# Ten of sixteen conditioning vectors are computed among the mixers' projections, each in two halves of 32 matmuls

## The chip, the cores and the metric

One core of a Trainium2 chip runs the program. The metric is the device time of one execution in microseconds (us); a table gives it for three executions, and one further execution was profiled. Engines are named as the profile names them: PE (TensorE matmuls) and PEld (its weight loads), DVE (VectorE), ACT (ScalarE), POOL (GpSimd), and SP, whose queue issues nearly all DMAs, in order.

## The reference

Two layers of a diffusion-transformer block over 512 latent and 256 context tokens of width 1024. Each layer has three sublayers: feed-forward, mixer (differential attention, a state-space scan and a retention scan side by side) and feed-forward. A conditioning vector `c` (and `c_ctx` for the context) yields nine vectors of width 1024 per layer: shift, scale and gate of each sublayer.

```python
sc, scc = silu(c), silu(c_ctx)
for l in range(2):
    m_l = (sc @ ada_w[l] + ada_b[l]).reshape(b, 1, 3, 3, D)      # 9 vectors for the latent tokens
    m_c = (scc @ ada_w[l] + ada_b[l]).reshape(3, 3, D)           # 9 for the context tokens
    x  = residual(x,  0.5 * swiglu(x * (1 + m_l[0, 1]) + m_l[0, 0], ...), gate m_l[0, 2])   # sublayer 0
    xc = ... the same with m_c
    y_l, y_c = hybrid_mixer(x * (1 + m_l[1, 1]) + m_l[1, 0], ...)                           # sublayer 1
    x = residual(x, y_l, gate m_l[1, 2])
    x = residual(x, 0.5 * swiglu(x * (1 + m_l[2, 1]) + m_l[2, 0], ...), gate m_l[2, 2])     # sublayer 2
    # the context stream has sublayers 1 and 2 in the first layer only
```

Here `residual` is a layer norm of `alpha * x + (1 + gate) * sublayer`. One vector is a product of a 1024 x 1024 block of `ada_w` with two columns (latent and context).

## The kernel before

Six sublayers follow each other: `ffn(0,0)`, `mixer(0)`, `ffn(0,2)`, `ffn(1,0)`, `mixer(1)`, `ffn(1,2)`. Tiles come from pools with a fixed number of buffers per tag; a scheduler orders each engine's instructions, and each engine then runs its own list in order and waits on semaphores.

**Feed-forward.** 22 column blocks are taken as 11 pairs in the groups (0,1), (2,3), (4,5), (6,7), (8,9,10). For a pair, the gate and up weights (1 MB each) are loaded into a buffer of the tag `raw` (two buffers of 1 MB), some sums of blocks are formed on POOL, and ACT and DVE split each block into two float16 pieces (lines L320 and L321). PE then runs the gate and up products (L511, or L571 where the pair is done plainly), and at a group's end the down products (L743; L816 for the last group). Feed-forward of layer 1's last sublayer is wholly plain (L571, L772, L816).

**Mixer.** Projections of the input, 256 columns at a time, are *fill*: generators in a queue of jobs (`Fill`), which a list of pipelined steps (`Skew`) runs in small portions between the steps of the scans and of attention. `share` is the portion per step, the jobs' summed cost over the number of steps. Weights of a projection come by `unit()`, two names ahead of their use, through the same two `raw` buffers, and are split into blocks of a ring of 16. Projections write PSUM tiles of the tag `pf` (two buffers). At the end `merge` multiplies with `w_out` (its four blocks are the units `wo0` to `wo3`, their matmuls L1566).

**Conditioning vectors.** `ada_vec(l, v)` computes one. The two columns sit in `scT`, padded to 32, as the stationary operand; 128 rows of `ada_w` by 1024 columns are loaded per `k` (512 KB, tag `ada`, two buffers), and four matmuls of 256 columns write the four 32-row strips of one PSUM tile (L162; each float32 matmul is two records in the trace). After eight `k`, gates (v of 2, 5, 8) go to DRAM as rows, and the others are transposed on PE and written to `mT` by DVE. Vectors 0 and 1 of layer 0 are done in `first_pair` (in blocks of 128 columns, L639). The other sixteen are in `plan`: seven in `ffn(0,0)` and nine in `ffn(0,2)`, one ahead of each pair's products. The scheduler puts their matmuls between others as their loads land.

Of the kernel before, what the change touches and what calls it, by code (L numbers as in the profile page):

```python
# [8 lines left out]
F32 = mybir.dt.float32  # L9
# [34 lines left out]
def kernel(  # L44
# [110 lines left out]
    def ada_vec(l, v, alloc):  # L155

        pa = sm([P, 256], f"ada{l}_{v}")
        for k in range(KC):
            raw = alloc([P, D], f"adaw{l}_{v}_{k}")
            nc.sync.dma_start(out=raw, in_=ada_w[l, k * P:(k + 1) * P, v * D:(v + 1) * D])  # L160
            for j in range(4):
                PE.matmul(pa[32 * j:32 * j + 32, :], lhsT=scT[:, k, :], rhs=raw[:, j * 256:(j + 1) * 256],  # L162
                          start=(k == 0), stop=(k == KC - 1), tile_position=(0, 32 * j))
        rows = small.tile([P, 256], F32, tag="adar", name=f"adar{l}_{v}", bufs=1)
        if v % 3 == 2:
            mul = ISC if v == 5 else 0.5 * ISC
            G.memset(rows, 0.0)
            for r in range(2):
                nc.sync.dma_start(out=rows[r::32, :],
                                    in_=ada_b[l, v * D:(v + 1) * D].rearrange("(j f) -> j f", j=4))  # L170
            V.tensor_tensor(out=rows, in0=pa, in1=rows, op=ALU.add)
            V.tensor_scalar(out=rows, in0=rows, scalar1=mul, scalar2=mul, op0=ALU.mult, op1=ALU.add)
            row = dram.tile([2, D], F32, name=f"grow{l}_{v}")
            for r in range(2):
                nc.sync.dma_start(out=row[r].rearrange("(j f) -> j f", j=4), in_=rows[r::32, :])
            gate_rows[l, v // 3] = row
            return
        V.tensor_copy(rows, pa)
        pt = sm([P, 2, P], f"adat{l}_{v}")
        for h in range(2):  # L180
            PE.transpose(pt[:, h, :], rows[:, h * P:(h + 1) * P], ident)
        src = pt.rearrange("p h (j m) -> p h j m", m=32)
        dst = mT[l][:, v, :, :].rearrange("p (j h) r -> p h j r", h=2)
        bias = ab_cols[:, l, v * 8:v * 8 + 8].rearrange("p (j h) -> p h j", h=2)
        for h in range(2):
            V.tensor_tensor(out=dst[:, h], in0=src[:, h, :, 0:2],
                            in1=bias[:, h].unsqueeze(2).to_broadcast([P, 4, 2]), op=ALU.add)
# [169 lines left out]
    def ffn(l, i, uT, stream, ntiles, nxt, last, todo):  # L357
# [5 lines left out]
        with tc.tile_pool(name=f"ffn{l}{i}", bufs=1) as fp:  # L363
# [487 lines left out]
            for gi, prs in enumerate(GROUPS):  # L851
                for q in prs:
                    if todo and (q > 1 or len(todo) >= NPAIR - 1 - q):
                        ada_vec(*todo.pop(0), al("ada"))
# [70 lines left out]
    def mixer(l, uT, stream, nxt, last):  # L925
# [5 lines left out]
        with tc.tile_pool(name=f"mix{l}", bufs=1) as mp:  # L931
# [57 lines left out]
            pipe = Skew(fill)  # L989

# [601 lines left out]
            fill.add(1.3, ret_kt(1))  # L1592
            share = fill.left / 13
# [6 lines left out]
            for pr_ in range(2):  # L1600
                for n, t in enumerate(order_f):
                    if (pr_, n) == (0, 3):
                        fill.add(nout * TOK, gate_job("z", gate_ssm))
                        fill.add(ROT, qk_job(0))
                    pipe.push(ret_state(pr_, t), share)
# [6 lines left out]
            for h in range(2, 4):  # L1612
                fill.add(ROT, qk_job(h))
            fill.add(nout * TOK, gate_job("rg", gate_ret))
            share = fill.left / (3 * nout + LEAD)
            for h in range(4):
                for t in range(nout):
                    pipe.push(attend(h, t), share)
                    if (h, t) == (3, LEAD - 1):
                        merge_setup()  # L1620
# [4 lines left out]
            pipe.drain()  # L1625
        return mg["norm"]
# [7 lines left out]
    plan = {(0, 0): [(0, v) for v in range(2, 9)], (0, 2): [(1, v) for v in range(9)]}  # L1634
# [73 lines left out]
```

## Time and profile before

| | |
|---|---|
| device time, three executions | 2879.3, 2877.5, 2873.37 us (median 2877.5) |
| the profiled execution | 2878.8 us, of which 2877.0 are the span from first to last instruction |
| PE busy | 2656.4 us, 92% of the span |
| DVE busy | 2118.9 us, 74% |
| ACT, POOL busy | 1210.6 and 1160.1 us, 42% and 40% |
| mean granted TensorE clock | 0.973 of full |

Busy time is the union of an engine's instructions over the span, and the sublayers differ in what limits them, so the shares are averages. A granted clock below 1 means that PE ran part of the time at the lower of its two levels, 1.2 instead of 2.4 GHz.

### The profile page before, as it was taken

The numbers are of one execution on the slowest core, as the hardware profiler recorded it, in microseconds if no ns is written. First come the engines' busy times: TensorE is split into PE (matmuls) and PEld (weight loads), VectorE is DVE, ScalarE is ACT, GpSimd is POOL, SyncE is SP. The second block draws the span as 40 slices with busy tenths as digits, with TensorE's granted clock in tenths as the row PEclk, the third lists the DMA queues.
The fourth block names the chain that finished last, engine by engine and source line by source line (L and its number), as shares of the span: only waits on it lengthen the run. The fifth ranks groups of instructions, "written<-read, shape, count | busy, mean of one in ns | idle before, by whom it ended". The sixth has DMA issues, their size and how long they took to land. (4 is left out here: it accounts for less than half of the span.)

```text
span 2877.0 us, 42905 instructions
## 1 busy us (share of the span) xinstructions
PE 2656.4 (92%) x16415; PEld 1554.0 (54%) x16415; DVE 2118.9 (74%) x3134; ACT 1210.6 (42%) x2619; POOL 1160.1 (40%) x1016
## 2 busy tenths in 40 slices
PE   6899999989899988999999889988999899899998
PEld 4454555557677863544555444544555667744443
DVE  4967788786867688768877988879787768634455
ACT  3443344434436444533443344433433537333321
POOL 1744465241525455534552655446242425400011
PEclk8999999999999999999999999999999999999999
DMA  7635432333234244444453422221422333152330
GB/s 242 196 127 176 133 132 98 107 121 90 78 88 105 74 176 163 160 161 147 147 169 121 165 65 82 74 66 61 156 83 87 103 107 100 67 176 88 120 122 30
DMA packets 220355, 342.63 MB, mean 119 GB/s; under 512 B 16008, under 2 KB 162166, under 8 KB 220150
## 3 DMA queue, kind: packets, MB, share of 16 engines
q1 hardware_dynamic: 220150, 339.90, 36.6%
q8 instruction: 129, 2.11, 0.3%
q14 instruction: 76, 0.62, 0.1%
HBM read 301.43 MB, written 23.22 MB: 113 GB/s over the span
## 5 line engine op out<-in xcount | busy, mean ns | idle before, releaser
L511 PEld LDWEIGHTS <-pcgu 128*128 128x128 f16 x3792 | 373.4, 99 | 329.1 <-issue 93.3
L511 PE MATMUL ch<-T,pcgu 128*128 128x384 f16 x1920 | 337.0, 329 | 5.2 <-ACT U L518 5.2
L743 PEld LDWEIGHTS <-act 128*128 128x128 f16 x1512 | 142.9, 98 | 216.4 <-issue 58.4
L321 DVE SCALAR_TENSOR_TENSOR pcgu<-rawgu,pcgu 128x512 f16<-128x512 f32 x218 | 216.3, 1008 | 49.2 <-ACT pcgu L320 48.2
L571 PE MATMUL pl<-uT,pcgu 128*128 128x512 f16 (+2 forms) x1068 | 228.0, 367 | 7.7 <-DVE uT L214 7.0
L320 ACT ACTIVATE pcgu<-rawgu 128x512 f16<-128x512 f32 x218 | 133.9, 626 | 211.5 <-PE ds L743 126.6
L429 POOL TENSOR_TENSOR S4gu<-rawgu,S2gu 128x512 f32<-128x512 f32 x60 | 90.1, 1502 | 273.7 <-DVE pcgu L321 137.3
L571 PEld LDWEIGHTS <-pcgu 128*128 128x128 f16 x1236 | 121.8, 101 | 138.5 <-issue 24.7
L511 PEld LDWEIGHTS <-pegu 128*128 128x128 f16 x1248 | 122.2, 98 | 108.2 <-issue 29.7
L800 POOL TENSOR_TENSOR acc<-acc,gate 128x512 f32<-128x512 f32 x44 | 62.2, 1421 | 282.9 <-DVE acc L780 253.7
L743 PE MATMUL ds<-pcd,act 128*128 128x512 f16 x612 | 152.3, 381 | 4.3 <-DVE acc L749 2.8
L743 PE MATMUL dc<-pcd,act 128*128 128x512 f16 x576 | 149.1, 384 | 7.2 <-DVE acc L749 7.1
L976 PEld LDWEIGHTS <-uT 128*128 128x128 f16 x1344 | 134.7, 101 | 29.9 <-issue 8.4
L228 ACT ACTIVATE u<-pt,abc 128x128 f32<-128x128 f32 x224 | 81.2, 467 | 161.2 <-PE pt L225 98.9
L816 PE MATMUL pd<-pcd,act 128*128 128x512 f16 x594 | 141.1, 379 | 4.2 <-DVE dt L822 4.2
L321 DVE SCALAR_TENSOR_TENSOR pcd<-rawd,pcd 128x512 f16<-128x512 f32 x124 | 109.0, 893 | 40.6 <-ACT pcd L320 40.5
L426 POOL TENSOR_TENSOR S1gu<-rawgu 128x512 f32<-128x512 f32 x60 | 88.8, 1480 | 116.2 <-DMA rawgu<-in_ffn_w_gate_dram 55.8
L816 PEld LDWEIGHTS <-act 128*128 128x128 f16 x792 | 77.4, 98 | 99.2 <-issue 10.7
L458 DVE TENSOR_TENSOR act<-sg,act 128x384 f16<-128x384 f32 (+1 forms) x149 | 123.6, 873 | 3.3 <-ACT act L457 3.3
L94 POOL TENSOR_SCALAR rs<-mv 128x1 f32<-128x1 f32 x32 | 17.9, 559 | 263.3 <-DVE mv L273 263.3
L518 ACT COPY U<-ch 128x384 f32<-128x384 f32 x180 | 83.6, 472 | 76.8 <-PE ch L511 76.1
L428 POOL TENSOR_TENSOR S3gu<-rawgu 128x512 f32<-128x512 f32 x60 | 96.4, 1607 | 32.4 <-DVE pegu L321 16.2
(391 smaller groups left out, 6209.5 us busy)
## 6 DMA issues: line engine op xcount, KB each, us to landing
adaw<-in_ada_w_dram SPq DMA_DIRECT2D x128, 512.0 KB
rawd<-in_ffn_w_down_dram SPq DMA_DIRECT2D x44, 1024.0 KB
rawgu<-in_ffn_w_gate_dram SPq DMA_DIRECT2D x43, 1024.0 KB
rawgu<-in_ffn_w_up_dram SPq DMA_DIRECT2D x43, 1024.0 KB
row<-yh SPq DMA_DIRECT2D x56, 256.0 KB
rawwo<-in_w_out_dram SPq DMA_DIRECT2D x8, 1024.0 KB
xt<-row SPq DMA_DIRECT2D x32, 256.0 KB
gate<-grow SPq DMA_DIRECT2D x28, 256.0 KB
```

The lines of the kernel that those rows point to most:

```text
L320: A.activation(pc[:, 0], src, AF.Copy, scale=SW)
L321: V.scalar_tensor_tensor(out=pc[:, 1], in0=src, scalar=SW, in1=pc[:, 0], op0=ALU.mult, op1=ALU.subtract)
L426: G.tensor_tensor(out=s1, in0=a21, in1=a22, op=ALU.add)
L428: G.tensor_tensor(out=s3, in0=a11, in1=a21, op=ALU.subtract)
L429: G.tensor_tensor(out=s4, in0=a12, in1=s2, op=ALU.subtract)
L458: V.tensor_tensor(out=pc[:, 1], in0=src, in1=pc[:, 0], op=ALU.subtract)
L511: PE.matmul(pp, lhsT=wt[pr_][q][m][:, a, k, :], rhs=rhs, start=(n == 0 and m in (1, 2, 5)), stop=(n == 11), skip_group_check=m in (1, 6, 7 ...
L518: A.copy(t_, chain[q])
L571: PE.matmul(pp[:, j, o:o + hi - lo], lhsT=wp.at(a, k, cc * P, (cc + 1) * P), rhs=uT[:, b, k, lo:hi], start=(n == 0), stop=(n == KC * 3 - 1))
L743: PE.matmul(pd, lhsT=acts[q][m][:, a, ts], rhs=wd[q][m][:, b], start=(n == 0 and m in (1, 2, 5)), stop=(n == len(prs) * 3 - 1), skip_group ...
L816: PE.matmul(pd, lhsT=acts[q][2 * cc + hf][:, a, o:o + P], rhs=wd[q][2 * cc + h][:, b], start=(n == 0), stop=(n == len(prs) * 6 - 1))
L976: PE.matmul(pp, lhsT=uT[:, a, k, t * P:(t + 1) * P], rhs=pc.at(b, k, 0, n_), start=(n == 0), stop=(n == KC * 3 - 1))
```

## The change

Three things change together. `ada_vec` becomes a generator that works on halves of 512 columns: per half all weights are loaded first (`nk` row blocks per DMA), then 32 matmuls of 128 columns follow each other, and then the half is finished. In the feed-forward sublayers it is run at once with `nk = 2` (DMAs of 512 KB in the two `ada` buffers). In the mixers it is a fill job with `nk = 4` (DMAs of 1 MB in the two `raw` buffers, PSUM in `pf`). And `plan` now gives three vectors to `ffn(0,0)`, six to `mixer(0)`, three to `ffn(0,2)` and four to `mixer(1)`.

```diff
-    def ada_vec(l, v, alloc):
-        pa = sm([P, 256], f"ada{l}_{v}")
-        for k in range(KC):
-            raw = alloc([P, D], f"adaw{l}_{v}_{k}")
-            nc.sync.dma_start(out=raw, in_=ada_w[l, k * P:(k + 1) * P, v * D:(v + 1) * D])
-            for j in range(4):
-                PE.matmul(pa[32 * j:32 * j + 32, :], lhsT=scT[:, k, :], rhs=raw[:, j * 256:(j + 1) * 256],
-                          start=(k == 0), stop=(k == KC - 1), tile_position=(0, 32 * j))
...
+    def ada_vec(l, v, alloc, space, nk):
         for h in range(2):
+            c0 = v * D + h * 512
+            raws = []
+            for k in range(0, KC, nk):
+                raws.append(alloc([P, nk, 512], f"adaw{l}_{v}_{h}{k}"))
+                nc.sync.dma_start(out=raws[-1], in_=ada_w[l, k * P:(k + nk) * P, c0:c0 + 512]
+                                  .rearrange("(k p) f -> p k f", p=P))
+            yield 0.5
+            pa = space([P, P], f"ada{l}_{v}{h}")
+            for k in range(KC):
+                for j in range(4):
+                    PE.matmul(pa[32 * j:32 * j + 32, :], lhsT=scT[:, k, :],
+                              rhs=raws[k // nk][:, k % nk, j * P:(j + 1) * P],
+                              start=(k == 0), stop=(k == KC - 1), tile_position=(0, 32 * j))
+            yield 1.7
...
# ffn
-                        ada_vec(*todo.pop(0), al("ada"))
+                        for _ in ada_vec(*todo.pop(0), al("ada"), sm, 2):
+                            pass
...
# mixer
+            raw_of = lambda shape, nm: main.tile(shape, F32, tag="raw", name=f"raw{nm}", bufs=2)
+            told = set()
+            def ada_job(v):
+                yield from ada_vec(*v, raw_of, pf, 4)
+                told.add(v)
+            def add_ada(n):
+                for _ in range(min(n, len(todo))):
+                    fill.add(4.4, ada_job(todo.pop(0)))
...
             fill.add(1.3, ret_kt(1))
+            add_ada(1)
...
                         fill.add(ROT, qk_job(0))
+                        add_ada(1)
...
             for h in range(2, 4):
+                add_ada(1)
                 fill.add(ROT, qk_job(h))
             fill.add(nout * TOK, gate_job("rg", gate_ret))
+            add_ada(len(todo))
...
                     if (h, t) == (3, LEAD - 1):
+                        fill.until(lambda: needed <= told)
                         merge_setup()
...
             pipe.drain()
+            fill.until(lambda: not fill.jobs)
...
-    plan = {(0, 0): [(0, v) for v in range(2, 9)], (0, 2): [(1, v) for v in range(9)]}
+    plan = {(0, 0): [(0, v) for v in range(2, 5)], (0, 1): [(0, v) for v in range(5, 9)] + [(1, 0), (1, 1)],
+            (0, 2): [(1, v) for v in range(2, 5)], (1, 1): [(1, v) for v in range(5, 9)]}
```

**In the feed-forward sublayers** the scheduler still breaks the runs up. On PE, in the down products of pairs 2 and 3 of `ffn(0,0)`, before (`ada_5` is vector 5, `adaw_5_1` its second load):

```order
L743 MATMUL dc_11_2121<-pcd_2_1_1755,act_2_1_1693 128x512
L162 MATMUL ada_5_2677<-adaw_5_1_2684,scT 32x256
L162 MATMUL ada_5_2677<-adaw_5_2_2690,scT 32x256 x3
L743 LDWEIGHTS act_2_2_1696
L743 MATMUL ds_10_2120<-pcd_2_2_1758,act_2_2_1696 128x512
```

and in the same place of the change (`ada_41` is the second half of vector 4, `adaw_4_14` its load from row block 4 on):

```order
L748 MATMUL ds_10_2197<-pcd_2_2_1799,act_2_2_1737 128x512
L169 MATMUL ada_41_2465<-adaw_4_14_2461,scT 32x128 x2
L169 MATMUL ada_41_2465<-adaw_4_16_2463,scT 32x128 x5
L748 LDWEIGHTS act_2_2_1737
L748 MATMUL ds_11_2199<-pcd_2_2_1799,act_2_2_1737 128x512
```

Vector 5 and those after it have left this place. Over the whole program the vectors' matmuls stood in 121 runs before (52 in `ffn(0,0)`, 69 in `ffn(0,2)`) and stand in 110 now (31, 28 in `mixer(0)`, 32 in `ffn(0,2)`, 19 in `mixer(1)`).

**In the first mixer** PE had, between the transposes of the retention keys (`rkp`) and the gate projection (`pkz`):

```order
L1310 MATMUL rkp_0_7119<-mats,rrrk_0_6566 128x128 x3
L1188 MATMUL pst_0_6596<-xw_0_6594,bt_6331 128x256 x2
L976 LDWEIGHTS uT_5049
L976 MATMUL pkz_0_7147<-pcz_6365,uT_5049 128x256
L976 LDWEIGHTS uT_5049
```

and has now, with the first vector that moved here (vector 5 of layer 0):

```order
L1329 MATMUL rkp_0_6937<-mats,rrrk_0_6449 128x128 x3
L169 MATMUL ada_50_6951<-rawadaw_5_00_6942,scT 32x128 x16
L169 MATMUL ada_50_6951<-rawadaw_5_04_6944,scT 32x128 x16
L169 MATMUL ada_51_7052<-rawadaw_5_10_7044,scT 32x128 x16
L982 LDWEIGHTS uT_4934
```

48 matmuls stand ahead of the projection that followed at once before; the vector's last 16 come among the scan's next steps.

**On SP, at the end of the first mixer,** the loads of the last `w_out` blocks (`rawwo`) and of the next sublayer's first weights (`rawgu`) stood like this before:

```order
L337 DMA rawwo_9508<-in_w_out_dram 128x8x256
L1410 DMA qs_0_9008<-rpaq_0_9005 64x768 x2
L337 DMA rawgu_00_10694<-in_ffn_w_gate_dram 128x8x256
L1417 DMA ks_0_9077<-rpak_0_9074 64x2x768 x4
L243 DMA gbc_0_9526<-agb 128x1024
L337 DMA rawgu_01_10708<-in_ffn_w_up_dram 128x8x256
L243 DMA bbc_0_9528<-agb 128x1024
```

and now, with the loads of layer 1's vectors 0 and 1 (`rawadaw_0_10` is the second half of vector 0):

```order
L243 DMA bbc_0_9926<-agb 128x1024
L163 DMA rawadaw_0_10_9699<-in_ada_w_dram 128x4x512
L163 DMA rawadaw_0_14_9701<-in_ada_w_dram 128x4x512
L163 DMA rawadaw_1_00_9768<-in_ada_w_dram 128x4x512
L163 DMA rawadaw_1_04_9770<-in_ada_w_dram 128x4x512
L163 DMA rawadaw_1_10_9831<-in_ada_w_dram 128x4x512
L1572 DMA xr_0_10030<-row_0_5062 128x1024
L163 DMA rawadaw_1_14_9833<-in_ada_w_dram 128x4x512
L342 DMA rawwo_9892<-in_w_out_dram 128x8x256
L1572 DMA xr_0_10212<-row_1_5146 128x1024
L342 DMA rawwo_9906<-in_w_out_dram 128x8x256
```

Six loads of vectors now stand between the norm's rows and the last two `w_out` blocks, all in the two `raw` buffers.

## Rows read from the trace of the kernel before

**Rows 1.** The page's first part: busy us, share of the span, instructions.

```profile
PE 2656.4 (92%) x16415; PEld 1554.0 (54%) x16415; DVE 2118.9 (74%) x3134; ACT 1210.6 (42%) x2619; POOL 1160.1 (40%) x1016
```

**Rows 2.** First and last starts of L743 and L816 in `ffn(1,0)`: ns min/median/max, starts.

```profile
L743 PE MATMUL dc<-pcd,act x180: 377/379/632, 1688.8 to 2008.7; 128*128 128x512 f16 x180
...
L816 PE MATMUL pd<-pcd,act x162: 377/379/380, 2058.0 to 2144.9; 128*128 128x512 f16 x162
```

**Rows 3.** Busy time by windows: `ffn(0,0)`, `ffn(0,2)`, `ffn(1,0)`, first down product to last.

```profile
core 0: us, PE busy (x) PEld busy (x) DVE busy (x) ACT busy (x) POOL busy (x), PEclk, DMA share, GB/s
130.10:593.70 463.60, 443.56 (x2635) 228.94 (x2633) 364.86 (x495) 199.53 (x386) 219.49 (x158) 1.00 0.40 130
1126.80:1600.40 473.60, 456.52 (x2789) 232.01 (x2787) 363.12 (x498) 191.81 (x371) 219.23 (x159) 0.99 0.46 151
1688.80:2145.30 456.50, 418.80 (x2267) 223.62 (x2265) 367.58 (x471) 190.65 (x374) 215.00 (x155) 0.98 0.25 81
```

**Rows 4.** The same three windows, matmuls of the tile `ada` alone.

```profile
130.10:593.70 463.60, 31.39 (x360) 1.00 0.40 130
1126.80:1600.40 473.60, 44.13 (x512) 0.99 0.46 151
1688.80:2145.30 456.50, 0.00 (x0) 0.98 0.25 81
```

**Rows 5.** PE's waits in `ffn(1,0)`, 1645 to 2009: us, times, longest.

```profile
PE dc L743 <- DVE acc L749: 10.5, 7, 2.8
```

**Rows 6.** PE's timeline around runs of vector matmuls: start us, us, count of records.

```profile
37.03 0.93 PE L685 MATMUL pc_first<-uT_in,pcfirst 128*128 128x256 f16 x7
37.89 0.30 PE L639 MATMUL ada_first<-pcadaw_first,sc 128*32 128x128 f32 x2
...
39.56 0.28 PE L639 MATMUL ada_first<-adaw_first,sc 128*32 128x128 f32 x2
39.77 0.39 PE L685 MATMUL pc_first<-uT_in,pcfirst 128*128 128x256 f16 x2
...
96.38 0.64 PE L162 MATMUL ada<-adaw,scT 128*32 128x256 f32 x8
96.95 4.08 PE L511 MATMUL ch<-uT_in,pcgu 128*128 128x384 f16 x24
...
172.40 1.07 PE L162 MATMUL ada<-adaw,scT 128*32 128x256 f32 x16
173.40 0.82 PE L743 MATMUL dc<-ped,act 128*128 128x512 f16 x3
```

**Rows 7.** Groups of instructions by shape: the vectors' matmuls and their transposes.

```profile
L162 PE MATMUL ada<-adaw,scT 128*32 128x256 f32 x1024 | 88.5, 394 | 1.9 <-DMA adaw<-in_ada_w_dram 1.6
...
L181 PE MATMUL adat<-mats,adar 128*128 128x128 f32 x20 | 3.8, 273 | 0.0
```

**Rows 8.** Windows: `mixer(0)`, `mixer(1)`, and two stretches of `mixer(0)` (columns as rows 3).

```profile
594.00:1031.60 437.60, 412.17 (x3061) 318.82 (x3059) 325.98 (x589) 209.50 (x563) 169.52 (x225) 0.98 0.32 93
2145.30:2512.00 366.70, 338.05 (x2406) 251.33 (x2405) 273.16 (x487) 176.59 (x453) 137.25 (x175) 0.97 0.33 97
...
918.00:958.30 40.30, 35.06 (x256) 27.61 (x256) 30.93 (x61) 34.40 (x107) 22.48 (x40) 1.00 0.26 79
...
736.00:760.00 24.00, 15.96 (x105) 13.42 (x104) 23.07 (x43) 11.98 (x36) 13.21 (x16) 0.85 0.35 111
```

**Rows 9.** PE's waits in the mixers (594 to 1031, then 2145 to 2512).

```profile
PE sc L1434 <- ACT pe L1439: 5.4, 6, 3.0
PE pch L1242 <- DVE yo L1232: 5.2, 2, 4.5
...
PE pl L571 <- DVE uT L214: 7.0, 1, 7.0
```

**Rows 10.** From the chain that ended last: landings of 1 MB weight loads.

```profile
2500.55 5.28 DMA rawgu<-in_ffn_w_gate_dram
...
2530.69 11.13 DMA rawd<-in_ffn_w_down_dram
```

More of the change, by code (lines that the diff above doesn't have):

```diff
@@ L152, in condition @@
         nc.sync.dma_start(out=agb.rearrange("r (k p) -> (r k) p", p=P), in_=agb_sb)
-    def ada_vec(l, v, alloc):
-        pa = sm([P, 256], f"ada{l}_{v}")
-        for k in range(KC):
-            raw = alloc([P, D], f"adaw{l}_{v}_{k}")
-            nc.sync.dma_start(out=raw, in_=ada_w[l, k * P:(k + 1) * P, v * D:(v + 1) * D])
-            for j in range(4):
-                PE.matmul(pa[32 * j:32 * j + 32, :], lhsT=scT[:, k, :], rhs=raw[:, j * 256:(j + 1) * 256],
-                          start=(k == 0), stop=(k == KC - 1), tile_position=(0, 32 * j))
[L164 to L179, printed above, removed]
-        for h in range(2):
[L181 to L187, printed above, removed]
@@ new lines, in ada_vec @@
+    def ada_vec(l, v, alloc, space, nk):
+        for h in range(2):
+            c0 = v * D + h * 512
[12 more added lines that the diff above has]
+            yield 1.7
+            rows = small.tile([P, P], F32, tag="adar", name=f"adar{l}_{v}{h}", bufs=2)
+            if v % 3 == 2:
+                mul = ISC if v == 5 else 0.5 * ISC
+                G.memset(rows, 0.0)
+                for r in range(2):
+                    nc.sync.dma_start(out=rows[r::32, :], in_=ada_b[l, c0:c0 + 512].rearrange("(j f) -> j f", j=4))
+                V.tensor_tensor(out=rows, in0=pa, in1=rows, op=ALU.add)
+                V.tensor_scalar(out=rows, in0=rows, scalar1=mul, scalar2=mul, op0=ALU.mult, op1=ALU.add)
+                if h == 0:
+                    gate_rows[l, v // 3] = dram.tile([2, D], F32, name=f"grow{l}_{v}")
+                for r in range(2):
+                    nc.sync.dma_start(out=gate_rows[l, v // 3][r, h * 512:(h + 1) * 512]
+                                      .rearrange("(j f) -> j f", j=4), in_=rows[r::32, :])
+                continue
+            V.tensor_copy(rows, pa)
+            pt = space([P, P], f"adat{l}_{v}{h}")
+            PE.transpose(pt, rows, ident)
+            V.tensor_tensor(out=mT[l][:, v, 4 * h:4 * h + 4, :], in0=pt.rearrange("p (j m) -> p j m", m=32)[:, :, 0:2],
+                            in1=ab_cols[:, l, v * 8 + 4 * h:v * 8 + 4 * h + 4].unsqueeze(2).to_broadcast([P, 4, 2]),
+                            op=ALU.add)
@@ L922, in drain, with mixer @@
                 self.push()
-    def mixer(l, uT, stream, nxt, last):
+    def mixer(l, uT, stream, nxt, last, todo):
         need_ctx = l < DEPTH - 1
@@ L989, in mixer @@
             pipe = Skew(fill)
+            raw_of = lambda shape, nm: main.tile(shape, F32, tag="raw", name=f"raw{nm}", bufs=2)
[6 more added lines that the diff above has]
+                    fill.add(4.4, ada_job(todo.pop(0)))
+            needed = set(q for q in todo if q[0] == l and q[1] < 8)
             sv = sml([P, 4, 2, 4], "sv")
@@ L1639 @@
         if i == 1:
-            norm = mixer(l, uT, stream, nxt, last)
+            norm = mixer(l, uT, stream, nxt, last, todo)
         else:
```

## Prediction

> **What bounds the kernel now.** The page's first part comes first: PE is busy for 92% of the span and DVE for 74% [rows 1]. That makes PE the suspect everywhere, but the vectors move from one kind of sublayer to another, so the question is what a microsecond of PE work costs in each kind. The trace holds a comparison made for this. `ffn(0,0)`, `ffn(0,2)` and `ffn(1,0)` have the same six token tiles and the same products, and carry seven, nine and no vectors. I marked the same stretch in each, from the first down product to the last (for `ffn(1,0)` the starts 1688.8 and 2144.9 of [rows 2], the others alike), and read it by windows. Without vectors the stretch takes 456.5 us, and PE is busy for only 418.8 of them [rows 3]: there PE waits again and again for DVE, most of all for sums into the accumulator [rows 5]. With 31.4 us of vector matmuls it takes 463.6 us, with 44.1 us of them 473.6 [rows 3, 4]. So the first 31.4 us cost 7.1 us, 0.23 for one, and the next 12.7 cost 10.0, 0.79 for one. A feed-forward sublayer has room for some of this work, and not for all that it has now.
>
> The mixers are the other side. PE is busy for 412.2 of 437.6 us in the first and 338.1 of 366.7 in the second [rows 8]: 25.4 and 28.6 us are not used, of which 7.0 are one wait at the very end of the second, for the next sublayer's input [rows 9].
>
> **What one vector costs on PE.** In the timeline a run of 8 records (four float32 matmuls of 256 columns, one for each strip) holds PE from 96.38 to 96.95, 0.57 us; a run of 16 holds it from 172.40 to 173.40, 1.00 [rows 6]. So four matmuls cost 0.43 us, and a run 0.14 beside. Ahead of a run PE loses a little more: seven matmuls of 256 columns take 0.86 us up to the run's start at 37.89 [rows 6], where 7 x 256 columns at 2.4 GHz are 0.75. A run thus costs about 0.24 us beyond its fours. A run of 32 matmuls of 128 columns stands in the trace too: 37.89 to 39.77, 1.88 us [rows 6]; less 0.14 and divided by eight, 0.218 us for a four. Half the columns, half the price.
>
> The number of fours comes from the order, incomplete ones counted whole, since their strips run side by side. Before: 64 fours in 52 runs in `ffn(0,0)` and 81 in 69 in `ffn(0,2)`, that is 40.0 and 51.4 us; the sum of 91.4 can be held against the 88.5 of [rows 7]. Now: 59 fours in 31 runs and 60 in 32 there, 20.3 and 20.8 us; 103 in 28 in `mixer(0)` and 69 in 19 in `mixer(1)`, 29.2 and 19.6 us. All of it is 89.9 us. The two runs of 32 are broken up by the scheduler, so hardly any PE time is saved; 50.3 us leave the feed-forward sublayers, and 48.8 arrive in the mixers. With them move 12 of the 20 transposes, at 0.19 us [rows 7], 2.3 us: the mixers get 51.1.
>
> A rule of the Trainium skill speaks against halving the columns. Its page "TensorE: Matmul & The Clock Gate", section "Back-to-back issue gap", gives a sustained spacing of about 81 ns for matmuls of 128 columns that each load their weights; by it the 2048 records of the changed kernel would take 166 us, an estimate, and the sum below would be larger by some 76 us. The row has 64 records in 1.74 us, 27 ns each, in tiles of 32 columns as here, and the measurement decides.
>
> **What the feed-forward sublayers give back.** About 13.5 us of vector work should stay in the marked stretch of `ffn(0,0)` and 17.5 in that of `ffn(0,2)`. At 0.2 us for one, near the cheap end of the curve, that leaves 2.7 and 3.5 of the 7.1 and 17.1 us that the vectors cost now [rows 3]. So 4.4 and 13.6 come back, and some 2 more for the 64 of the 576 records of `ffn(0,2)` that stand ahead of the marked stretch (17.1 x 64 / 512): 20 us. If the rest costs nothing it is 26; if the vectors' cost falls only in proportion, 4.1 + 10.3 + 2, about 16. As `ffn(1,0)` need not be the floor of the other two, I keep 14 to 26.
>
> **What the mixers pay.** No row shows a vector in a mixer, so this is bounded. At the rates of the feed-forward sublayers (0.23, and 17.1 / 44.1 = 0.39) 51.1 us cost 12 to 20; if none of it meets a gap, 51. I take a value between. The 7.0 us at the end and what lies ahead of the first fill job are out of reach; I count that as a third of the 54 us, which leaves 36. The jobs sit in the queue in a fixed place and not where a wait is, so I count half, 18 us. The best case is the stretch 736 to 760 [rows 8], where PE is busy for 16.0 of 24.0 us while scan steps wait for DVE, one of them 4.5 us [rows 9], and where the clock is 0.85; the first moved vector lands there. For the clock, 0.98 and 0.97 over the mixers, I count another 4 us. The mixers pay 51.1 - 18 - 4 = 29 us.
>
> **What I cost at nothing.** DVE's copies and sums for a vector are done in halves and keep their columns; in the mixers DVE is busy for 74% [rows 8], and its slack covers them; without that cover, a wait such as those of [rows 5] (10.5 us in 7, 1.5 each) at every one of the ten is 15 us. The loads' 40 MB move with the vectors, and DMA is used to a third in the mixers. The one new resource is the pair of `raw` buffers: vectors and projection weights now wait for each other in it. Units are asked for two names ahead, which hides a turn of the ring, except at the end of the first mixer, where four halves follow each other and the last two `w_out` blocks come behind them on SP. From the first half of layer 1's vector 0 to the block `wo2` the ring turns four times, each a landing of 5.28 to 11.13 us [rows 10] and sixteen matmuls, 1 us: 25 to 49 us. On PE stand meanwhile, counted from the order, about half of the 35.1 us of attention and merge work that the stretch 918 to 958 has [rows 8], 7 us of vector halves and the first half of a tile's output products, 5 us: 29. So 0 to 20 us; with a DMA share of 0.26 there, the short landing is the nearer one, and I take 0.
>
> **The sum.** 29 - 20 = +9 us on the profiled execution's 2878.8 (span 2877.0 and 1.8 around it). The median of the runs lies 1.3 lower, so 2886 us.
>
> **Rivals.** *The mixers absorb like the feed-forward sublayers do.* For it speaks that `Fill` exists to fill gaps and that 54 us of gap face 51 of work; against it, that these gaps remained although fill was at hand. At 0.23 the mixers pay 12: 2878.8 - 1.3 + 12 - 20 = 2869, faster. It decides below 14 us, 28% of the inserted work.
>
> *The ring of two `raw` buffers becomes the wait.* At the long landing the end of the first mixer loses 20 us, and `qs`, `ks` and rows queue behind the waiting loads on SP: 2886 + 12 to 20, 2898 to 2906. Against it, the short landing leaves 4 us to spare.
>
> *A record of 128 columns costs as much as one of 256.* Then 291 fours at 0.43 instead of 0.218 add 62 us: 2948. The row at 37.89 speaks against it. The page named above would give such a direction.
>
> *The move cancels itself,* 2877: PE work is the same, and it would need the same price on both sides.
>
> **Chances.** Forecast 0.43 (2879 to 2897; 0.32 of it slower, 0.11 within 0.2%), absorbing mixers 0.37 (0.28 faster, 0.09 within), ring 0.13, dear records 0.02, cancelling 0.05. About 0.2%, 5.8 us, is what a measurement of this kernel can tell from no change. So faster 0.28, same 0.25, slower 0.47. The range leaves out the lowest and highest tenth: 2866 (26 us given back, 14 paid) to 2906 (the ring's 20 us on top of the forecast).
>
> **What will show it.** In the changed kernel a run of 32 vector matmuls should hold PE for 1.9 us, and all of them about 90. The marked stretch of `ffn(0,0)` should take 459 us, that of `ffn(0,2)` 460, that of `ffn(1,0)` 456 as now. `mixer(0)` should grow by some 17 us and `mixer(1)` by 12, with PE busy for about 97%. A PE wait for `rawadaw` or for `pcwo` at the end of the first mixer would be the ring. The prediction is wrong if the mixers grow by under 14 us together, or by over 40, or if the feed-forward sublayers give back under 14.

## The result, and the profile after

The changed kernel takes 2948.8 us (median of four runs, 2940.63 to 2954.66), the kernel before 2875.4 in runs beside it: 1.0255 times as long, 95% interval 1.022 to 1.029. The forecast was 2886 in a range of 2866 to 2906, so it is wrong by more than its range. The profiled execution took 2940.63 us, of which 2938.6 are the span; it is the shortest of the four, 8 us under their median. Below, "us against before" is a ratio's excess times 2877 us, so that runs made beside different runs of before can be compared; the change is +73 us.

The page's first part, and the groups of the vectors' matmuls (`rawadaw` are those in the mixers), to be held against [rows 1, 7]:

```profile
PE 2668.5 (91%) x17439; PEld 1591.9 (54%) x17439; DVE 2143.8 (73%) x3156; ACT 1210.3 (41%) x2619; POOL 1154.7 (39%) x1022
...
L169 PE MATMUL ada<-rawadaw,scT 128*32 128x128 f32 x1280 | 52.3, 295 | 21.2 <-DMA rawadaw<-in_ada_w_dram 21.2
L169 PE MATMUL ada<-adaw,scT 128*32 128x128 f32 x768 | 39.5, 285 | 4.7 <-DMA adaw<-in_ada_w_dram 4.7
```

PE is busy for only 12.1 us more than before, and the span is 61.6 us longer: most of the new time is PE standing still. The last column says where some of it is: 21.2 us ahead of the mixers' vector matmuls, spent waiting for their own loads. Windows (columns as in [rows 3]) of `ffn(0,0)`, `ffn(0,2)`, `ffn(1,0)` from first down product to last, of `mixer(0)` and `mixer(1)`, and of the stretch 736 to 760, against [rows 3, 8]:

```profile
130.70:591.80 461.10, 430.12 (x2509) 229.14 (x2507) 366.54 (x482) 198.72 (x386) 216.58 (x158) 0.99 0.30 97
1146.70:1616.10 469.40, 435.12 (x2623) 231.55 (x2621) 374.02 (x487) 192.10 (x372) 221.18 (x162) 0.99 0.32 105
1702.20:2160.50 458.30, 420.38 (x2266) 224.01 (x2265) 371.43 (x473) 191.42 (x374) 217.25 (x157) 0.98 0.25 80
591.80:1057.80 466.00, 440.39 (x3837) 339.20 (x3836) 331.76 (x622) 210.19 (x563) 170.85 (x229) 0.99 0.45 142
2160.50:2574.20 413.70, 366.01 (x2921) 269.67 (x2920) 280.37 (x507) 177.27 (x453) 136.48 (x177) 0.95 0.42 127
...
736.00:760.00 24.00, 23.92 (x219) 20.53 (x217) 22.42 (x43) 15.66 (x43) 14.04 (x14) 1.00 0.81 260
```

The same windows for the tile `ada` alone (PE busy and records only), against [rows 4]:

```profile
130.70:591.80 461.10, 13.24 (x238) 0.99 0.30 97
1146.70:1616.10 469.40, 17.94 (x352) 0.99 0.32 105
...
591.80:1057.80 466.00, 29.18 (x768) 0.99 0.45 142
2160.50:2574.20 413.70, 23.12 (x512) 0.95 0.42 127
```

So the two stretches that lost 18.2 and 26.2 us of vector work became only 2.5 and 4.2 us shorter; `mixer(0)` grew by 28.4 us and `mixer(1)`, which got a third less work than `mixer(0)`, by 47.0. In the first, PE's idle time is 25.6 us, as before (25.4), so all of the inserted work was paid. It is not the same idle time: of the waits for ACT and DVE in [rows 9], 5.4 and 5.2 us, the first is gone and the second is 1.1 us, and 8.6 us are now waits for the vectors' loads. In the second mixer the idle time rose from 28.6 to 47.7. PE's waits in the mixers (592 to 1058, then 2160 to 2574, against [rows 9]; us, times, longest), and last what SP's queue waits for in the second:

```profile
PE ada L169 <- DMA rawadaw<-in_ada_w_dram: 8.6, 7, 4.5
...
PE ada L169 <- DMA rawadaw<-in_ada_w_dram: 12.6, 5, 6.8
...
PE att L1475 <- ACT po L1487: 3.2, 3, 2.6
...
SPq L163 <- PE ada L169: 48.1, 7, 19.8
```

The last line says that SP stands for 48.1 us at loads of vectors, until PE has done the vector matmuls that free their buffers. In the first mixer it is 59.0 us, so this standing does not by itself cost PE time. PE's timeline around the longest wait in the first mixer and, after the first dots, in the second, columns as in [rows 6]; in brackets the idle time before the row:

```profile
724.90 1.95 PE L169 MATMUL ada<-rawadaw,scT 128*32 128x128 f32 x64
731.33 1.94 PE L169 MATMUL ada<-rawadaw,scT 128*32 128x128 f32 x32 [4.47 <-DMA rawadaw<-in_ada_w_dram]
...
2429.24 7.96 PE L972 MATMUL pjak<-uT,pcak 128*128 128x512 f16 x48
...
2437.36 1.08 PE L169 MATMUL ada<-rawadaw,scT 128*32 128x128 f32 x32
...
2451.51 1.93 PE L169 MATMUL ada<-rawadaw,scT 128*32 128x128 f32 x32 [6.82 <-DMA rawadaw<-in_ada_w_dram]
2455.45 1.94 PE L169 MATMUL ada<-rawadaw,scT 128*32 128x128 f32 x32 [2.02 <-DMA rawadaw<-in_ada_w_dram]
2457.32 1.90 PE L972 MATMUL pjaq<-uT,pcaq 128*128 128x512 f16 x6
```

and SP's queue beside the second of them (start, us of issuing, transfer, count):

```profile
2428.75 0.37 SPq L163 DMA_DIRECT2D rawadaw<-in_ada_w_dram  x1
2432.33 5.01 SPq L1286 DMA_DIRECT2D swaq<-rraq  x8
2437.44 4.96 SPq L1286 DMA_DIRECT2D swak<-rrak  x8
2442.49 2.45 SPq L1429 DMA_DIRECT2D qs<-rpaq  x4
2444.99 2.25 SPq L163 DMA_DIRECT2D rawadaw<-in_ada_w_dram  x2
```

Sixteen matmuls of a vector (32 records) run at 2437.36; the loads for the next are issued at 2444.99, behind twenty small transfers of rotated queries and keys. PE takes its list in order: it reaches those matmuls and stands for 6.8 us, though projections are next in the list. In the first mixer it stands for 4.5 us between the two halves of the first vector that moved there.

### The profile page after: what moved, and what is told of

The parts are those of the page before. It is cut to its first block, busy times and chain, and to the rows that moved or that the text cites. A ratio compares the mean times of both kernels' runs of the same rounds, so it can differ in the third digit from the quotient of the medians.

```text
span 2938.6 us, 44913 instructions
## 1 busy us (share of the span) xinstructions
PE 2668.5 (91%) x17439; PEld 1591.9 (54%) x17439; DVE 2143.8 (73%) x3156; ACT 1210.3 (41%) x2619; POOL 1154.7 (39%) x1022
## 3 DMA queue, kind: packets, MB, share of 16 engines
q1 hardware_dynamic: 236086, 339.90, 35.6%
## 5 line engine op out<-in xcount | busy, mean ns | idle before, releaser
L576 PEld LDWEIGHTS <-pcgu 128*128 128x128 f16 x1236 | 120.9, 101 | 137.2 <-issue 22.5
L94 POOL TENSOR_SCALAR rs<-mv 128x1 f32<-128x1 f32 x32 | 17.9, 561 | 265.8 <-DVE mv L278 265.8
L1585 PE MATMUL pm<-pcwo,mT 128*128 128x256 f16 x960 | 108.4, 275 | 0.0
```

What stands on the lines that cost most here:

```text
L576: PE.matmul(pp[:, j, o:o + hi - lo], lhsT=wp.at(a, k, cc * P, (cc + 1) * P), rhs=uT[:, b, k, lo:hi], start=(n == 0), stop=(n == KC * 3 - 1))
L1585: PE.matmul(pm[:, q * 256:(q + 1) * 256], lhsT=mT_[k // 4][:, a, k % 4, :], rhs=wo[2 * hf + q].at(b, k, 0, 256), start=(n == 0), stop=(n = ...
```

## Experiments

Every run is told against before; 95% intervals in brackets. By these intervals the difference of two runs is good to some 7 to 12 us. Three questions: what do vectors cost in the feed-forward sublayers, what does the halving cost, and what of the mixers' price is PE work and what is loads.

Windows show where time goes, but they come from one execution each, and they repeat only so far. `mixer(0)` without vectors took 437.6 us in [rows 8], and in the profiles of six whole and of six halved vectors (first two lines); `ffn(1,0)`, which has no vectors before either, took 456.5 us in [rows 3], and in the profile with no planned vector (last line):

```profile
592.70:1024.60 431.90, 409.73 (x3062) 318.14 (x3060) 326.00 (x593) 210.37 (x563) 174.66 (x225) 0.99 0.32 95
598.80:1042.20 443.40, 416.38 (x3062) 320.54 (x3060) 327.36 (x593) 209.86 (x563) 168.03 (x225) 0.97 0.31 92
...
1656.70:2120.60 463.90, 425.31 (x2267) 225.29 (x2265) 369.83 (x472) 191.28 (x374) 217.76 (x157) 0.96 0.25 79
```

So up to 12 us in `mixer(0)` and 7 in a feed-forward stretch can come without any change of the work, and the 2.5 and 4.2 us above lie within that. `mixer(1)` without vectors stayed between 364.2 and 366.7 us in five profiles.

**No planned vector at all.** Columns are zeroed and gates are constants, so that the rest runs as it is.

```diff
+    for l in range(DEPTH):
+        G.memset(mT[l], 0.0)
...
-    plan = {(0, 0): [(0, v) for v in range(2, 9)], (0, 2): [(1, v) for v in range(9)]}
+    plan = {}
```

> The kernel before with all sixteen planned vectors left out (shift and scale columns are zero and gates a constant instead). It shows the floor of the three stretches. If ffn(1,0)'s 456.5 us is the floor of the other two, as the prediction took it, ffn(0,0) takes 456 to 458, ffn(0,2) 456 to 460, and the program some 26 us less than before, 2850. The rival: these two sublayers are longer for another reason, and the vectors cost them less than the comparison said; then 461 and 466, and the program is only 8 to 14 us faster, 2862 to 2868.

0.9923 [0.9902, 0.9945], -22 us. All sixteen vectors cost 22 us in the kernel before, for 88.5 us of PE work: 0.25 for one, close to what the comparison of stretches said (26). No more than this can be had by moving them out of the feed-forward sublayers.

**Six whole vectors.** The plan of the change without its ten in the mixers, with the old routine; zeros and constants stand for the ten.

```diff
...
-    plan = {(0, 0): [(0, v) for v in range(2, 9)], (0, 2): [(1, v) for v in range(9)]}
+    plan = {(0, 0): [(0, v) for v in range(2, 5)], (0, 2): [(1, v) for v in range(2, 5)]}
```

> The kernel before with its old routine for a vector (whole vectors, 256 columns per matmul) and only the three vectors in each of ffn(0,0) and ffn(0,2) that stay there in the change; the ten others are left out. Before minus this is what the ten cost in the feed-forward sublayers. The prediction's curve says 20 us: 2856. What the changed kernel's stretches show (461.1 and 469.4 us) says about 5 to 13 us: 2863 to 2870.

0.9942 [0.9923, 0.9962], -17 us. The ten cost 17 us in the feed-forward sublayers; the forecast had 20. The group of the six, for comparison with the next run:

```profile
L162 PE MATMUL ada<-adaw,scT 128*32 128x256 f32 x384 | 35.2, 410 | 3.2 <-DMA adaw<-in_ada_w_dram 3.2
```

**Six halved vectors.** The same plan line in the changed kernel.

> The changed kernel with the ten vectors of the mixers left out; the six of the feed-forward sublayers stay, in halves. Against the run with six whole vectors it shows what halving costs there: nothing by the prediction (within 3 us), up to 10 us if two halves with copies, transposes and loads of their own disturb more. The changed kernel minus this is what ten vectors cost in the mixers: about 75 us by the windows (28 in the first mixer, 47 in the second), so 2873 or less.

0.9993 [0.9981, 1.0005], -2 us. So halving six vectors takes back 15 of the 17 us.

```profile
L169 PE MATMUL ada<-adaw,scT 128*32 128x128 f32 x768 | 39.9, 286 | 8.0 <-DMA adaw<-in_ada_w_dram 8.0
```

PE work grows by 4.7 us, the wait for loads by 4.8. The clock is hardly the rest: this profile has a mean of 0.967 and that of the run before 0.972, but over all executions the means are 0.970 in both. How the rest divides is not settled; in these two profiles `mixer(0)` is 11.5 us longer with halves (431.9 and 443.4 above), with no vector in it either time. And the changed kernel minus this one, 75 us (64 to 86), is what ten vectors cost in the mixers.

**All sixteen halved, none moved.** The changed kernel with the plan line of before.

> The changed kernel with the plan of before: all sixteen vectors in the feed-forward sublayers, in halves, none in the mixers. Six halved vectors took 14 us more than six whole ones. If halving costs by the vector, sixteen cost 38 us: 2916. If the 14 us were chance or belong to the first vectors of a sublayer only, 2878 to 2892; the prediction's step (halves cost PE the same) says 2878.

1.0071 [1.0046, 1.0095], +20 us. The clock is no part of it here (0.974, before 0.973). The vectors' group, and the stretches of `ffn(0,0)` and `ffn(0,2)`:

```profile
L169 PE MATMUL ada<-adaw,scT 128*32 128x128 f32 x2048 | 102.9, 284 | 20.5 <-DMA adaw<-in_ada_w_dram 20.5
...
129.30:598.40 469.10, 450.49 (x3024) 239.19 (x3023) 373.99 (x501) 199.25 (x386) 212.87 (x160) 1.00 0.41 131
1131.00:1616.30 485.30, 465.45 (x3301) 246.51 (x3299) 369.89 (x510) 192.83 (x371) 217.25 (x162) 0.99 0.46 147
```

PE spends 102.9 us instead of 88.5 [rows 7]. By the order of PE's records the vectors' matmuls now stand in 166 runs where 121 were (75 for 52, and 91 for 69); 45 more at the forecast's 0.24 us each are 10.8 us, most of the 14.4. The idle time ahead of them rises from 1.9 to 20.5 us. The two stretches are 5.5 and 11.7 us longer than in [rows 3], which is about what the whole span grew by (15.9).

**Moved, but whole.** The change's plan; whole vectors everywhere, in the mixers as fill jobs in the same places, two 1 MB loads at a time.

```diff
...
+            elif k % 4 == 0:
+                for k2 in (k, k + 2):
+                    raw = alloc([P, 2, D], f"adaw{l}_{v}_{k2}")
...
+                yield 0.5
             for j in range(4):
-                PE.matmul(pa[32 * j:32 * j + 32, :], lhsT=scT[:, k, :], rhs=raw[:, j * 256:(j + 1) * 256],
+                PE.matmul(pa[32 * j:32 * j + 32, :], lhsT=scT[:, k, :], rhs=raws[k][:, j * 256:(j + 1) * 256],
                           start=(k == 0), stop=(k == KC - 1), tile_position=(0, 32 * j))
+            if nk == 2 and k % 4 == 3:
+                yield 1.7
...
```

> The change's plan with whole vectors everywhere (256 columns per matmul, as before); in the mixers they are fill jobs in the same places, each with two pairs of 1 MB loads in the raw buffers. The move without the halving. PE work per vector is about the same, so the mixers should pay about as in the changed kernel. If halving costs 14 us in the feed-forward sublayers and nothing in the mixers: 2935. If it also costs in the mixers (by the vector, 2.4 us): 2912. The prediction, which costs the halving at nothing, has 2949 for this as for the change, once its result is known.

1.0141 [1.0117, 1.0166], +41 us. The move alone is slower, and the halving beside it makes up the other 32: 15 of them are the six vectors above, and the windows put the rest in the mixers. The two mixers here:

```profile
589.30:1050.40 461.10, 441.96 (x3454) 329.04 (x3452) 330.55 (x614) 210.36 (x563) 173.95 (x227) 0.99 0.45 143
2157.90:2558.10 400.20, 361.16 (x2665) 258.81 (x2664) 277.64 (x501) 176.71 (x453) 138.31 (x176) 0.97 0.42 131
```

They grow by 23.5 and 33.5 us, 18 less in sum than with halves, and the second mixer is the dearer one with whole vectors too.

**The mixers' loads left out.** All matmuls of the mixers' vectors stay, on the identity matrix.

```diff
+                if nk == 4:
+                    continue
...
-                              rhs=raws[k // nk][:, k % nk, j * P:(j + 1) * P],
+                              rhs=ident if nk == 4 else raws[k // nk][:, k % nk, j * P:(j + 1) * P],
```

> The changed kernel with the loads of the mixers' vectors left out: all their matmuls stay, but read the identity matrix that is in SBUF anyway. Theory of waiting (PE stands in order at vector matmuls for their 1 MB loads, and weights of projections queue behind those in the two raw buffers): 30 to 45 us come back, 2903 to 2918, with the first mixer near 450 and the second near 385 us. Theory of work (a mixer cannot absorb PE work, each us costs one): at most the 21 us that PE waits for rawadaw come back, and PE busy time keeps the mixers at 460 and 400: 2930 or more.

1.0152 [1.0129, 1.0174], +44 us: 30 come back, at the edge of what the theory of waiting expected, and 45 of 75 stay. The windows of `mixer(0)` and `mixer(1)` say where:

```profile
592.10:1062.30 470.20, 442.49 (x3837) 341.19 (x3836) 330.60 (x622) 211.00 (x563) 170.09 (x229) 0.99 0.30 87
2171.10:2562.30 391.20, 361.84 (x2923) 265.34 (x2921) 276.68 (x507) 176.81 (x453) 133.18 (x177) 0.97 0.31 91
```

The first mixer is no shorter without loads (470.2, with them 466.0): in place of the 8.6 us of waits for them, PE now waits 5.8 us for DVE's `yssm` and 5.8 for the transfer of `ks`. The second loses 22.5 us, most of it idle time: 29.4 instead of 47.7. The other part of the 30 us has no place in these windows: this profile lies 8 us above the median of its executions, and that of the changed kernel 8 below.

**Three of four matmuls left out,** loads kept, in the mixers:

```diff
-            for k in range(KC):
+            ks = range(KC) if nk == 2 else (0, 4)
+            for k in ks:
...
```

> The changed kernel with three of four matmuls of the mixers' vectors left out: of each 1 MB load only the first row block is multiplied (8 matmuls per half). All loads, copies and transposes stay. Theory of work: the mixers take about 39 us less PE work and give nearly all of it back, 2910 to 2915. Theory of loads (the raw buffers hold the mixers up): the loads' 29 us stay and what matmuls cost was waiting, so no more than 15 us come back, 2934 or more.

1.0153 [1.013, 1.0175], +44 us: 29 come back, between the two forecasts. The same two windows:

```profile
594.40:1047.10 452.70, 423.15 (x3262) 324.51 (x3260) 327.71 (x622) 209.82 (x563) 170.95 (x229) 0.98 0.47 146
2155.60:2557.90 402.30, 353.71 (x2537) 257.05 (x2536) 277.81 (x507) 176.45 (x453) 135.78 (x177) 0.95 0.42 130
```

The second mixer is still 35.6 us longer than before with a quarter of the matmuls, and PE stands for 48.6 us in it. The next run, without the loads as well, takes 24.1 us of that away.

**Both cuts:** no loads, and a quarter of the matmuls.

> Both cuts of the two runs before at once: in the mixers no loads of vectors, and of each half only 8 of 32 matmuls (on the identity matrix). Copies, transposes and gate rows stay. Without loads, three quarters of the matmuls are some 39 us of PE work. If the mixers pay for PE work one for one, this is 39 us under the run without loads: 2880, and loads and matmuls add up (29 and 39 of the 75). If a mixer absorbs part of the work, less: 2890 to 2905.

1.0038 [1.0023, 1.0052], +11 us. The same windows:

```profile
592.20:1040.80 448.60, 420.78 (x3263) 323.78 (x3260) 330.60 (x622) 210.68 (x563) 173.50 (x229) 0.99 0.31 91
2145.50:2523.70 378.20, 345.95 (x2539) 255.72 (x2537) 279.73 (x507) 176.64 (x453) 136.48 (x177) 0.96 0.32 94
```

Without loads, three quarters of the matmuls are worth 44 - 11 = 33 us (25 to 41). Their PE time, three quarters of 52.3, is 39 us: 0.84 us for one (0.65 to 1.04). With loads it was 29 for 39. And the loads are worth 22.5 us in the second mixer with all matmuls and 24.1 with a quarter; in the first, -4.2 and 4.1, which that window varies by anyway. So the 75 us of the mixers are some 30 for loads, 33 for three quarters of the matmuls, and 13 for the last quarter with the copies, transposes and gate rows.

**Loads from another queue.** The timeline above suggests that on SP loads and small transfers hold each other up, so POOL, and in another run ACT (`nc.scalar` in place of `nc.gpsimd`), issues the mixers' vector loads.

```diff
-                nc.sync.dma_start(out=raws[-1], in_=ada_w[l, k * P:(k + nk) * P, c0:c0 + 512]
+                (nc.gpsimd if nk == 4 else nc.sync).dma_start(out=raws[-1], in_=ada_w[l, k * P:(k + nk) * P, c0:c0 + 512]
```

> The changed kernel with the loads of the mixers' vectors issued by POOL instead of SP; the same raw buffers, the same matmuls. In the second mixer PE stands 6.8 us at a vector whose load was issued behind twenty small transfers of rotated queries and keys on SP. Theory of the queue (loads and small transfers hold each other up on SP): most of the second mixer's 20 us of waiting go, 2925 to 2932, unless POOL's own work now waits behind the loads. Theory of the buffers (each half takes both raw buffers, so a half's loads wait for the half before, whoever issues them): no change, 2945 to 2950; a loss, if POOL stands at a load that waits for a buffer.

> The same with ACT as the issuer. Theory of the queue: 2925 to 2932. Theory of the buffers: 2945 to 2950, or above it, since a load that waits for a buffer then holds up what ACT has to do next (exponentials, splits of weights), by up to the 48 us that SP stands for vector buffers in the second mixer.

POOL: 1.0296 [1.0281, 1.0311], +85 us, worse than the change by 12 (the intervals just meet). ACT: 1.0252 [1.0232, 1.0272], +73, the same. The windows and PE's waits in `mixer(1)` with ACT:

```profile
592.20:1066.20 474.00, 443.75 (x3839) 340.11 (x3836) 329.87 (x622) 210.72 (x563) 171.66 (x229) 0.98 0.45 140
2174.60:2582.70 408.10, 367.19 (x2922) 270.74 (x2921) 282.76 (x507) 176.74 (x453) 134.96 (x177) 0.95 0.42 129
...
PE att L1475 <- ACT po L1487: 6.6, 4, 4.0
PE ada L169 <- DMA rawadaw<-in_ada_w_dram: 3.9, 3, 2.2
```

With ACT, PE's direct wait for vector loads falls from 12.6 to 3.9 us in the second mixer, which is 5.6 us shorter, but the wait for ACT doubles, and the first mixer is 8.0 us longer, within what that window varies by. In sum nothing comes back, so SP's queue is not the cause of the whole. How much of it is the queue stays open, since the new issuer can now stand at loads that wait for a buffer; POOL does so for 15.6 us in the second mixer.

**Every second load left out:** a half loads 1 MB, holds one `raw` buffer and multiplies it twice.

```diff
+                if nk == 4 and k == 4:
+                    raws.append(raws[0])
+                    continue
```

> The changed kernel with every second load of the mixers' vectors left out: a half loads 1 MB instead of 2 and multiplies it twice, so that it holds one of the two raw buffers and leaves the other to the weights. All 32 matmuls stay. Without any loads the kernel was 30 us faster. Theory of the buffers (a half that takes both shuts the weights out): most of the 30 us come back, 2920 to 2930. Theory of the landing (each half's matmuls stand behind one load's landing, however many there are): little comes back, 2940 or more. If only the bytes count: half, 2934.

1.0156 [1.0135, 1.0176], +45 us: 28 of the 30 us of all loads come back with half of them. If bytes counted it would be 1.0203, halfway between the ratios with all loads and with none, outside the interval; the landing theory (2940 or more) falls too. So what costs is the second load of a half. That a half then takes both buffers is the likeliest reason; that two loads landing side by side slow each other down was not separated from it (the DMA share is 0.97 in the stretch from 2451.50, shown at the end). The windows agree: the second mixer is as without loads (391.2), the first as with them.

```profile
592.40:1058.10 465.70, 439.83 (x3838) 338.69 (x3836) 331.78 (x622) 209.70 (x563) 174.74 (x229) 0.99 0.38 115
2161.10:2553.40 392.30, 361.28 (x2922) 265.86 (x2921) 278.78 (x507) 176.06 (x453) 135.58 (x177) 0.97 0.37 112
```

**Halves apart.** Each half is a fill job of its own, with a projection between it and the next as far as they go round.

```diff
-                    fill.add(4.4, ada_job(todo.pop(0)))
+                    fill.add(2.2, ada_job(*parts.pop(0)))
...
+            add_ada(1 if need_ctx else 0)
             fill.add(NT * TOK, av_job(0))
...
+            add_ada(1)
             fill.add(nout * TOK, gate_job("rg", gate_ret))
```

> The changed kernel with the two halves of a vector no longer one behind the other in the mixers: each half is a fill job of its own, with a projection between it and the next as far as there are enough of them. Same loads, same matmuls. Theory of the buffers with halves back to back as the worst place: 10 to 20 us come back, 2930 to 2940. If each half costs its share wherever it stands, no change: 2945 to 2952.

1.0225 [1.0203, 1.0247], +65 us. That is 9 less than the change, but the two intervals overlap, and less than the theory of halves back to back expected.

```profile
594.90:1076.50 481.60, 448.51 (x3839) 342.67 (x3836) 327.50 (x622) 210.49 (x563) 174.32 (x229) 0.97 0.44 137
2182.50:2582.30 399.80, 365.26 (x2922) 268.88 (x2921) 277.29 (x507) 176.31 (x453) 133.23 (x177) 0.96 0.43 131
```

In the second mixer the theory holds (399.8 instead of 413.7, idle 34.5 instead of 47.7). The first is 15.6 us longer, but this profile is the longest of its four executions (2951.29 us, median 2943.17), so that is not safely a price of the edit.

**Vectors in a sublayer that has none.** Before, with five of layer 1's vectors in `ffn(1,0)`.

```diff
-    plan = {(0, 0): [(0, v) for v in range(2, 9)], (0, 2): [(1, v) for v in range(9)]}
+    plan = {(0, 0): [(0, v) for v in range(2, 9)], (0, 2): [(1, v) for v in range(4)],
+            (1, 0): [(1, v) for v in range(4, 9)]}
```

> The kernel before, whole vectors, but five of layer 1's vectors (4 to 8) move from ffn(0,2), which has nine, to ffn(1,0), which has none; no vector in a mixer. Six vectors cost about 6 us over none and the next ten 18. If the price rises with the number in one sublayer, spreading them saves 4 to 10 us: 2868 to 2874. If every vector costs the same wherever it stands in a feed-forward sublayer, no change: 2878.

0.9998 [0.9986, 1.001], no difference. The steep end of the price curve in [rows 3, 4], 0.79 for one, does not show in the whole.

**Fewer runs.** Before, with loads of two row blocks (1 MB, one buffer) instead of one (512 KB, two buffers), so that eight matmuls stand ready at a time. Two rows of the norm, which had the two buffers, share the one.

```diff
-            raw = alloc([P, D], f"adaw{l}_{v}_{k}")
-            nc.sync.dma_start(out=raw, in_=ada_w[l, k * P:(k + 1) * P, v * D:(v + 1) * D])
+            if k % 2 == 0:
+                raw2 = alloc([P, 2, D], f"adaw{l}_{v}_{k}")
+                nc.sync.dma_start(out=raw2, in_=ada_w[l, k * P:(k + 2) * P, v * D:(v + 1) * D]
+                                  .rearrange("(k p) f -> p k f", p=P))
+            raw = raw2[:, k % 2, :]
...
-            ft = Tags(fp, act=14, ada=2, pcd=NEXTRA, xa=NT, bc=4, T=4, pt=6, sg=4)
+            ft = Tags(fp, act=14, ada=1, pcd=NEXTRA, xa=NT, bc=4, T=4, pt=6, sg=4)
...
```

> The kernel before with the plan and the whole vectors of before, but each load in a feed-forward sublayer brings two row blocks (1 MB in one buffer in place of two of 512 KB), so that eight matmuls stand ready at once. The runs fall from 121 to about 95 and PE work by 26 x 0.24 = 6 us. If PE time in these sublayers is worth 0.4 to 0.8 of itself, 2 to 5 us faster: 2872 to 2875. If one buffer makes each load wait for the products before it: slower, 2880 to 2890.

0.9968 [0.9957, 0.998], -9 us: faster than both kernels, and by more than the 2 to 5 us expected. The vectors' group, and the windows of `ffn(0,0)` and `ffn(0,2)`:

```profile
L165 PE MATMUL ada<-adaw,scT 128*32 128x256 f32 x1024 | 80.1, 395 | 6.9 <-DMA adaw<-in_ada_w_dram 6.9
...
127.80:591.70 463.90, 441.55 (x2656) 229.32 (x2655) 363.49 (x494) 198.50 (x386) 219.94 (x158) 1.00 0.40 134
1119.30:1584.60 465.30, 448.67 (x2790) 233.32 (x2789) 364.13 (x499) 192.88 (x371) 217.92 (x161) 1.00 0.46 155
```

The runs fall to 90 and PE's work for vectors by 8.4 us; `ffn(0,2)`, the fuller one, gives back 8.3 us, `ffn(0,0)` nothing. The same with five vectors in `ffn(1,0)`:

> The version with loads of 1 MB in one buffer, which was 9 us faster than before, with five of layer 1's vectors moved from ffn(0,2) to ffn(1,0). With the loads of before that move changed nothing. If that holds here too: 2866. If the last vectors of ffn(0,2) are still the dear ones: 2860 to 2864.

0.997 [0.9958, 0.9982], -9 us: again no gain from spreading.

## Why the prediction was wrong

**PE time of the vectors: right in total.** 52.3 + 39.5 = 91.8 us against 89.9 forecast, and 64 records of 32 matmuls take 1.95 us (724.90 in PE's timeline) against 1.88. The Trainium skill's page "TensorE: Matmul & The Clock Gate", section "Back-to-back issue gap", would have made it 166 us, an estimate; the measurement decides. The result lies where the rival of dear records put it, 2948, but not by its mechanism: PE is busy for 12 us more, not 62.

**What the feed-forward sublayers give back: right for the move, lost to the halving.** The curve from the three stretches gave 20 us, and ten whole vectors taken out give 17. That is partly luck, since the curve's steep end did not show when five vectors were spread. The step that failed is "At 0.2 us for one, near the cheap end of the curve", which was taken over for vectors in halves. Six whole vectors cost 5 us more than none (-17 against -22), 0.15 for one us of their 35.2; six halved ones cost 20, 0.5 for one of their 39.9, and all sixteen halved 42, 0.41 for one. PE's work in the two stretches was foreseen well (13.5 and 17.5 us, measured 13.2 and 17.9). What had no term is the longer wait for a half's loads, 8.0 us instead of 3.2 for six vectors and 20.5 instead of 1.9 for sixteen. So 2 us come back in place of 20. (In the profiles alone the mixers grow by 75.4 us and the span by 61.6, so 14 come back; the medians are the better measure.)

**What the mixers pay: the step that failed most.** Forecast 29 us, measured 75; by the prediction's own signs, a growth of over 40 is wrong. PE is busy there for 94.5 and 88.5% of the time, not 97. Of the 46 us that were missed some 30 are the loads, told below, and the rest is "I count half, 18 us" of the gaps as filled, and 4 for the clock. The run without loads has 27.7 and 29.4 us of idle time in the mixers, where before had 25.4 and 28.6: none of the gap was used in sum. By the medians PE work costs 0.84 of itself there (0.65 to 1.04), not 0.57. The stretch 736 to 760 did fill as foreseen (23.9 of 24.0 us busy, the clock at 1.00), but PE stood for 4.5 us just ahead of it, at 731.33. One reading fits, and no run tests it by itself: fill is a queue, and what goes in ahead of a projection pushes that projection later, out of the gap that it filled before.

**The raw buffers at nothing.** "Units are asked for two names ahead, which hides a turn of the ring, except at the end of the first mixer": the exception was the wrong one. At that end PE waits for a vector's load for 1.3 us at most. By the windows the first mixer pays nothing for loads, and the second 22.5 us. Its attention has four token tiles instead of six, and so less PE work between the turns; that this is why is argued and not tested. The rival of the ring came nearest, but in the wrong mixer and at 12 to 20 us instead of 30.

**DVE and the clock.** DVE is busy for 73%, and the largest new wait for it in the mixers is 3.7 us (PE's matmuls `pch`, in the second). The second mixer's clock is 0.95 where it was 0.97; the clock was taken as a gain of 4 us over both mixers, and became a loss in this one.

Not settled: how the 15 us of six halved vectors divide beyond PE's 4.7 and the wait's 4.8; where the part of the 30 us of loads lies that the second mixer's window doesn't show; and whether the second load of a half costs by the buffer that it takes, by its landing or by its place in a queue. A run with buffers of their own for the mixers' vectors, which would test the ring with all loads in place, was not made.

## What to carry to other kernels

Idle time of an engine is not safely room for work that joins a queue whose other items could fill the gaps already: here such work cost 0.84 of itself, so price it near its full time. Where a new consumer joins a ring of two buffers and takes both at a time, ask in every sublayer how much other work stands between two turns; here the mixer with fewer vectors and less work paid. And where small matmuls are broken up by others, count the runs: two loads joined into one gave 9 us here, while move and halving together cost 73, and the move alone 41.

## What the runs showed of the hardware

Runs of 32 records of a vector's half take 1.08 us at 2437.36, right behind busy work, and 1.93 us at 2451.51, behind a wait of 6.8 us. The windows of the two (PE busy, granted clock) show the clock's lower level, 1.2 instead of 2.4 GHz, in the second:

```profile
2437.40:2438.40 1.00, 1.00 (x32) 1.00 0.27 60
2451.50:2453.40 1.90, 1.90 (x32) 0.50 0.97 290
```

The 32 records at 731.33, behind a wait of 4.5 us, took 1.94 us, with a granted clock of 0.50 as well; those at 971.52, behind 1.1 us, took 1.08. So the long waits here were paid a second time in the work behind them.

There is another side that I had not expected: the kernel without vectors has a lower clock. Its four executions have means of 0.965 to 0.969, the thirteen of before beside them 0.973 to 0.977. The stretches of `ffn(0,0)` and `ffn(0,2)` in it, with columns as above, the second at 0.97 instead of 0.99:

```profile
131.80:583.70 451.90, 415.23 (x2267) 222.88 (x2265) 363.63 (x469) 197.15 (x386) 218.12 (x156) 0.99 0.25 81
1109.90:1570.60 460.70, 423.00 (x2266) 224.56 (x2265) 371.47 (x470) 190.59 (x372) 221.81 (x160) 0.97 0.25 82
```

PE's other work in `ffn(0,2)` took 423.0 us without vectors and 412.4 beside them (456.5 less 44.1). This fits vector matmuls in PE's gaps that keep the clock up and so cost less than their own time (0.25 us for one). It was not tested by itself, and one row speaks against it as the whole cause: `ffn(1,0)`, with no vector in either kernel, fell from 0.98 to 0.96 in the same two profiles.
